# The first layer's 1/rms moved from the projections' input to their output

## The chip, the cores and the metric

The kernel runs on one core of one Trainium2 chip. The metric is the device time of one execution in microseconds; the median of 3 runs of the kernel before is 2711.04 (2710.79 to 2717.03). Everything is fp32 in and out. A core has five engines that run side by side, each with its own in-order stream: PE (TensorE, matrix products), DVE (VectorE), ACT (ScalarE), POOL (GpSimd) and SP, which here only issues DMAs. PE writes its products to PSUM, eight banks of 512 fp32 columns for each of 128 partitions.

## The reference, cut to what matters

A two-layer encoder trunk works on 1024 prompt frames and 64 sample frames of width 1024. Each layer adds a mixer and an FFN to x, and both read a normalised x:

```python
def rmsnorm(x, g):
    xf = x.astype(F32)
    y = xf * lax.rsqrt(jnp.mean(xf * xf, axis=-1, keepdims=True) + EPS) * g.astype(F32)
    return y.astype(x.dtype)

aq, ak, av, bq, bk, bv = split_cols(h @ w_in, AB_SIZES)     # h = rmsnorm(x, g)
```

The first layer's mixer has 4 heads of differential attention and 8 heads of band attention; queries, keys and values of all of them are columns of one projection of h. The 1/rms of a frame is one number per row of h, so it can be multiplied to a row of h @ w_in as well as to a row of x. New keys and values are outputs too.

## The kernel before, in words

Frames lie along the free axis, and model columns along the partitions, so x is 8 tiles of 128 rows by 1088 frames, cut into three chunks of 384, 384 and 320 frames (CH). A fp32 matrix is multiplied in two parts: ACT rounds it to a high part (L235) and DVE or POOL subtracts to get the low part (L236, `split`). One projection of 128 columns over one chunk is then 8 blocks of k times three products (L263 to L265 in `gemm`, L275 in `gemm_steps`, where they can be taken in pieces): high times high, high times low and low times high.

The first layer runs 8 units, one per differential head and one per pair of band heads. Each unit needs its own queries, keys and values: three projections over three chunks. Unit 0's are made in `start`, before any attention; those of units 1 to 7 are made by `proj`, as filler between the attention steps of the unit before, with two PSUM banks in turn. The parts of the normalised x, `hh` and `hl`, stay in SBUF for all of them.

`start` loads x chunk by chunk. For a chunk, `addsq` squares each of the 8 tiles on ACT (L300, L303) and sums them on DVE (L304); `rms` averages over partitions with a product with a constant matrix (L285) and takes 1/rms as exp(-0.5 ln(.)) on ACT (L289 or L291, and L292); `norm` multiplies x by the norm's weight and 1/rms on DVE (L313) and splits the result. The weights of keys and values are issued behind the first chunk's last low part. Then come the projections of a chunk and their unloading: `put_q` writes scaled high parts of the queries on ACT (L351, L352), copies them to the other half of the partitions by DMA and makes low parts on DVE (L356); `new_k` copies PSUM to a staging tile on DVE (L369) and splits it by halves (L332 to L335); `new_v` copies PSUM (L379), transposes on PE (L385) and splits. L487 and L488 are the score products, L499 to L502 the softmax, L520 its scaling, L604 the transposes of the weights.

The program is written in an order, but each engine's stream is laid out by a scheduler that takes ready instructions by its own estimate of times; `issue_after` holds instructions behind a named one. So DMAs and small work can stand far ahead of their place in the text. Buffers are fixed slices of three large tiles, and work that reuses a slice waits for its last reader. The staging tiles share space with the first chunk's sum of squares and with the scratch for squares; the scratch also with the cached keys.

Of the kernel before, what the change touches and what calls it, by code (L numbers as in the profile page):

```python
# [16 lines left out]
F32 = mybir.dt.float32  # L17
AF = mybir.ActivationFunctionType
ALU = mybir.AluOpType
# [5 lines left out]
CH = ((0, 384), (384, 384), (768, 320))  # L25
# [39 lines left out]
F_END = 14464  # L65
F_LF = 14464
F_STG2 = 15808

GROUPS = [(12064 + 2176 * i, 544) for i in range(4)] + [(7360, 544), (38720, 544), (9536, 544), (4416, 544)] + \
    [(R_H + 4 * T * i, T) for i in range(4)] + [(0, 544), (2176, 544)]  # L70
# [74 lines left out]
class Kernel:  # L145
    def __init__(self, tc, M, MR, PS, xTd, oTd, ed, fd, hd, I, O):
# [9 lines left out]
        self.pvp = Ring(PS, [3584], 512)  # L156
        self.mmd = self.mmf
        self.sq = None
        slots = lambda ii: Ring(MR, [R_W + 1024 * i for i in ii], 1024)
        self.raw = Ring(M, [F_RAW, F_RAW + 1024], 1024)  # L160
        self.w_a = slots([0, 1]), slots([2, 3])
# [114 lines left out]
            yield "z", n * 1.25e-3  # L276


    def rms(self, ci, parts=None, to=None):
        nc = self.nc  # L280
        c0, n = CH[ci]
        ms = self.mm.get()[:, :n]
        parts = parts or [ci]
        for p in parts:
            nc.tensor.matmul(ms, self.o1024, self.acc[p][:, :n], start=(p == parts[0]), stop=(p == parts[-1]))  # L285
        r = (self.rb.get() if to is None else to)[:, :n]
        if ci == 0:
            with self.tc.issue_after(self.table("natural_log_exp_and_others")):
                nc.scalar.activation(r, ms, AF.Ln, bias=self.eps)  # L289
        else:  # L290
            nc.scalar.activation(r, ms, AF.Ln, bias=self.eps)  # L291
        self.after_rms = nc.scalar.activation(r, r, AF.Exp, scale=-0.5).ins  # L292
        return r
# [53 lines left out]

    def put_q(self, d, c0, n, ps):
        nc = self.nc
        q0, q1, l0, l1 = (t[:, c0:c0 + n] for t in (*d["q"], *d["ql"]))  # L350
        nc.scalar.activation(q0[0:64], ps[0:64], AF.Copy, scale=SCALE)  # L351
        nc.scalar.activation(q1[64:128], ps[64:128], AF.Copy, scale=SCALE)  # L352
        self.dma(q0.bitcast(F32)[64:128], q0.bitcast(F32)[0:64])
        self.dma(q1.bitcast(F32)[0:64], q1.bitcast(F32)[64:128])
        for b, q, ql in ((0, q0, l0), (64, q1, l1)):
            nc.vector.scalar_tensor_tensor(ql[b:b + 64], ps[b:b + 64], SCALE, q.bitcast(F32)[b:b + 64], op0=ALU.mult, op1=ALU.subtract)  # L356

    def new_rows(self, c0, n, sg, outs, keep):

# [6 lines left out]

    def new_k(self, d, c0, n, ps, outs, keep, sub=None):
        sg = self.stg.get()[:, :n]
        self.nc.vector.tensor_copy(sg, ps)  # L369
        npr = min(n, TP - c0)  # L370
        self.put_k(d["k"], c0, ps[:, :npr], sg[:, :npr], npr, sub)
        if npr < n:
            self.put_k(d["ks"], PAST, ps[:, npr:n], sg[:, npr:n], TS, sub)
        self.new_rows(c0, n, sg, outs, keep)

    def new_v(self, d, c0, n, ps, pair, outs, keep):
        nc = self.nc
        sg = self.stg.get()[:, :n]
        nc.vector.tensor_copy(sg, ps)  # L379
        npr = min(n, TP - c0)  # L380
        nt = npr // 128
        yield "t", 0.0
        pt = self.ptp.get()
        for t in range(nt):
            nc.tensor.transpose(pt[:, t * 128:t * 128 + 128], sg[:, t * 128:t * 128 + 128], self.ident)  # L385
        self.put_v(d["v"], 8, c0 // 128, nt, 128, pt[:, :npr], pair, nc.vector)
        if npr < n:
            nc.tensor.transpose(pt[0:64, 384:512], sg[:, npr:n], self.ident)
            self.put_v(d["vs"], 3, 2, 1, 64, pt[:, 384:512], pair, nc.vector)
        self.new_rows(c0, n, sg, outs, keep)  # L390
# [40 lines left out]
    def start(self, d, wq, wk, wv, pair, outs):  # L431
        nc, I = self.nc, self.I
# [2 lines left out]
        rings = tuple(Ring(self.MR, [R_W + 2048 * i + o for i in range(2)] + [R_Q[1] + o], 1024) for o in (0, 1024))  # L435
        ring = Ring(self.PS, [512 * i for i in range(5)], 512)

        def loadx(ci):
            c0, n = CH[ci]
            for k in range(8):  # L440
                self.dma(self.x[k][ci], I["xT"][k * 128:k * 128 + 128, c0:c0 + n])

        loadx(0)
        w = [self.loadw(wq, rings)]
        loadx(1)
        for k in range(8):
            self.addsq(0, k, self.x[k][0])
        last = self.norm(0, 0, 1, (nc.gpsimd, nc.gpsimd))
        with self.tc.issue_after(last.ins):
            w.append(self.loadw(wk, rings, sub=nc.vector))  # L450
            w.append(self.loadw(wv, rings))
        loadx(2)
        self.dma(self.ident, I["ident"])
        self.dma(self.causal, I["causal"])
        for ci, (c0, n) in enumerate(CH):
            p = [ring.get()[:, :n] for _ in range(3)]
            for i in range(3):
                self.gemm(p[i], w[i], c0, n)
                if i == 0 and ci < 2:
                    self.norm(ci + 1, 0, 2 if ci == 0 else None)  # L460
            self.put_q(d, c0, n, p[0])
            if ci == 0:
                self.cached_k(d, ckT)
# [1049 lines left out]
    def layer_cd(self, pending):  # L1513
        nc, I, O = self.nc, self.I, self.O
        W = I["cdw"]
        self.lastu = 3
        rest = self.recurrent(pending, self.qkv_views(0), W[0], W[4], I["cckT"][0], (O["c_kT"][0], O["sc_kT"][0]), 0)
        self.dg = Ring(self.M, [F_BIAS + 2688 + 128 * i for i in range(3)], 128)
        units = [(W[u], W[4 + u], W[8 + u], True,
# [108 lines left out]
```

## Time and profile before

| | us |
|---|---|
| median of 3 runs | 2711.04 |
| profiled execution, its own time | 2712.83 |
| span of that execution | 2711.0 |
| PE busy in the span | 2596.9 (96%) |
| DVE busy | 1325.7 (49%) |
| ACT busy | 1196.2 (44%) |
| POOL busy | 1155.1 (43%) |
| mean granted PE clock | 0.987 |

The span runs from the first to the last instruction in the profile; the execution's own time lies a little around it. A row of a grouped view reads: line, engine, operation, what is written <- what is read, shape, count | busy time, mean ns of one | idle time of the engine just before, with what ended it. A timeline row begins with start and duration in us, and a bracket gives the idle time before it and what ended it. "banks" is PSUM; "arena" and "split_arena" are the two SBUF tiles.

### The profile page before, as it was taken

The page shows a single profiled execution, that of the slowest core. Times are in us where ns is not written, and L with a number is a line of the kernel's source. Part 1 is how long each engine was busy: PE and PEld are TensorE (multiplying, and loading weights), DVE is VectorE, ACT ScalarE, POOL GpSimd, SP SyncE. Part 2 cuts the span into 40 slices and gives each one's busy share as a digit, 9 for nine tenths or more (in the row PEclk, how much of TensorE's full clock was granted, in tenths as well). Part 3 has the DMA queues.
Part 4 walks back from the last instruction along what each step waited for, and adds up shares of the span by engine and source line. Part 5 has one row for each costly group of instructions (what it writes and reads, how often), then busy time and mean ns, then how long its engine had stood idle before and what let it go on. Part 6 is the DMA issues. An engine that isn't in the chain of part 4 may idle for free. (4 is left out here: it accounts for less than half of the span.)

```text
span 2711.0 us, 44897 instructions
## 1 busy us (share of the span) xinstructions
PE 2596.9 (96%) x17610; PEld 2525.3 (93%) x17610; DVE 1325.7 (49%) x2763; ACT 1196.2 (44%) x2373; POOL 1155.1 (43%) x939
## 2 busy tenths in 40 slices
PE   6999999999999999999998979999999999999998
PEld 5899999889899999999998969988989999999998
DVE  7666666777432333422156557777743233242214
ACT  5666667764322233311135566686432323331112
POOL 5222222324666666422335433343366666641230
PEclk9999999999999999999999989999999999999999
DMA  6222222342222222442232342234322122244211
GB/s 204 73 71 69 78 63 62 104 151 92 83 95 66 81 72 87 141 154 72 74 105 60 52 80 79 78 123 150 100 86 97 64 82 70 88 141 153 72 55 67
DMA packets 115109, 250.21 MB, mean 92 GB/s; under 512 B 21432, under 2 KB 70848, under 8 KB 114896
## 3 DMA queue, kind: packets, MB, share of 16 engines
q1 hardware_dynamic: 114896, 247.33, 29.9%
q8 instruction: 138, 2.26, 0.4%
q14 instruction: 75, 0.61, 0.1%
HBM read 179.09 MB, written 65.43 MB: 90 GB/s over the span
## 5 line engine op out<-in xcount | busy, mean ns | idle before, releaser
L236 POOL TENSOR_TENSOR split_arena<-arena,split_arena 128x512 fp32r<-128x512 f32 (+5 forms) x501 | 756.7, 1522 | 1181.6 <-ACT split_arena L235 1091.7
L1070 PE MATMUL banks<-split_arena 128*128 128x272 f32 x7392 | 944.5, 290 | 23.3 <-ACT arena L1077 8.0
L1070 PEld LDWEIGHTS banks<-split_arena 128*128 128x128 f32 x7392 | 937.6, 190 | 30.0 <-ACT arena L1077 8.8
L235 ACT ACTIVATE split_arena<-arena 128x512 fp32r<-128x512 f32 (+10 forms) x664 | 458.8, 707 | 1020.3 <-PE banks L1070 291.9
L275 PE MATMUL banks<-split_arena 128*128 128x384 f32 (+1 forms) x3384 | 632.0, 333 | 3.4 <-POOL split_arena L236 2.3
L275 PEld LDWEIGHTS banks<-split_arena 128*128 128x128 f32 x3384 | 558.5, 189 | 10.9 <-POOL split_arena L236 2.9
L1182 PE MATMUL banks<-split_arena 128*128 128x384 f32 (+1 forms) x1056 | 345.1, 327 | 2.2 <-DVE arena L1148 1.4
L1184 PE MATMUL banks<-split_arena 128*128 128x384 f32 (+1 forms) x1056 | 344.4, 326 | 0.0
L1183 PE MATMUL banks<-split_arena 128*128 128x384 f32 (+1 forms) x1056 | 344.2, 326 | 0.0
L236 DVE TENSOR_TENSOR split_arena<-banks,split_arena 128x512 fp32r<-128x512 f32 (+4 forms) x312 | 167.4, 541 | 89.9 <-ACT split_arena L235 87.2
L499 DVE CUSTOM_DVE_ANT_0 arena<-banks,arena 128x384 f32<-128x384 f32 (+4 forms) x368 | 175.5, 493 | 56.4 <-PE banks L488 40.2
L1182 PEld LDWEIGHTS banks<-split_arena 128*128 128x128 f32 x1056 | 198.2, 188 | 3.6 <-DVE arena L1148 2.0
L1183 PEld LDWEIGHTS banks<-split_arena 128*128 128x128 f32 x1056 | 198.2, 188 | 0.3
L1184 PEld LDWEIGHTS banks<-split_arena 128*128 128x128 f32 x1056 | 198.2, 188 | 0.0
L235 ACT ACTIVATE split_arena<-banks 128x512 fp32r<-128x512 f32 (+4 forms) x312 | 146.7, 476 | 97.4 <-PE banks L604 43.3
L236 DVE TENSOR_TENSOR split_arena<-arena,split_arena 128x1088 fp32r<-128x1088 f32 (+8 forms) x163 | 154.0, 952 | 70.9 <-ACT split_arena L235 70.4
L1081 DVE TENSOR_TENSOR arena<-banks,arena 128x544 f32<-128x544 f32 (+1 forms) x46 | 32.2, 700 | 301.7 <-PE banks L1070 301.7
L501 ACT ACTIVATE arena<-arena 128x640 f32<-128x640 f32 (+8 forms) x216 | 156.3, 724 | 47.0 <-DVE arena L499 45.5
L1214 DVE TENSOR_TENSOR arena<-banks,arena 128x384 f32<-128x384 f32 (+1 forms) x96 | 51.1, 534 | 250.4 <-PE banks L1184 250.2
L604 PE MATMUL banks<-arena 128*128 128x128 f32 (+2 forms) x828 | 135.4, 276 | 18.8 <-DVE arena L520 11.5
L604 PEld LDWEIGHTS banks<-arena 128*128 128x128 f32 (+2 forms) x828 | 96.4, 141 | 37.7 <-DVE arena L520 15.1
L263 PE MATMUL banks<-split_arena 128*128 128x384 f32 (+1 forms) x312 | 106.7, 344 | 16.7 <-ACT arena L1399 10.0
(165 smaller groups left out, 3076.4 us busy)
## 6 DMA issues: line engine op xcount, KB each, us to landing
arena<-in_w_dram SPq DMA_DIRECT2D x120, 512.0 KB, 3.6
h_spill<-arena SPq DMA_DIRECT2D x22, 1088.0 KB, 4.2
arena<-h_spill SPq DMA_DIRECT2D x44, 544.0 KB, 4.4
arena<-in_abw_dram SPq DMA_DIRECT2D x24, 512.0 KB, 3.6
arena<-in_cdw_dram SPq DMA_DIRECT2D x20, 512.0 KB, 3.6
x_spill<-arena SPq DMA_DIRECT2D x48, 192.0 KB, 1.9
arena<-x_spill SPq DMA_DIRECT2D x16, 544.0 KB, 4.9
arena<-in_w_dram SPq DMA_DIRECT2D x19, 384.0 KB, 3.2
```

The lines of the kernel that those rows point to most:

```text
L235: self.hi = self.nc.scalar.activation(hi, x, AF.Copy).ins
L236: lo = sub.tensor_tensor(lo, x, hi.bitcast(F32), op=ALU.subtract)
L263: nc.tensor.matmul(ps, wh[:, k], hh[k][:, c0:c0 + n], start=(k == ks[0]), stop=False)
L275: self.pe = self.nc.tensor.matmul(ps, x[:, k], y[k][:, c0:c0 + n], start=a and i == 0, stop=z and i == 2).ins
L499: nc.vector.tensor_tensor_reduce(o, p, t, -1.0, low, ALU.add, ALU.min, to)
L501: nc.scalar.activation(sb, sb, AF.Exp, bias=st[:, 0:1], scale=-1.0, accum_out=st[:, 1:2])
L604: nc.tensor.transpose(pt[:r, t * nq + s * m:t * nq + s * m + m], src, self.ident[:m, :m])
L1070: last = nc.tensor.matmul(bank[:, p], l[:, k], r[:, k, x], start=first and i == 0, stop=k == 3 and i == 2, skip_group_check=True)
L1182: nc.tensor.matmul(ps, wh, h[:, c0:c0 + n], start=j == j0, stop=False)
L1183: nc.tensor.matmul(ps, wh, lo[:, c0:c0 + n], start=False, stop=False)
L1184: nc.tensor.matmul(ps, wl, h[:, c0:c0 + n], start=False, stop=j == j1 - 1)
L1214: nc.vector.tensor_tensor(xs, pss[ci], xs, op=ALU.add)
```

## The change

In the first layer, `hh` and `hl` become the parts of x times the norm's weight, without 1/rms. `parts` makes them: ACT writes the rounded product with a per-partition scale, DVE makes the low part in one scalar_tensor_tensor. 1/rms of each chunk is kept in a tile `rs` of its own (128 x 1088, at F_R, the place of the first buffer for raw FFN weights) and multiplied when a projection leaves PSUM: in place in PSUM for queries, in place of the copy for keys and values (`unload`). The key parts are then made from the staged copy. This holds for all 8 units; the second layer sets `rs` to None and unloads as before.

`start` is rearranged: weights of queries, half of x, weights of keys, the other half, weights of values, then the second and third chunk; the weights' low parts go to DVE instead of POOL. In the first chunk, the products of queries and of keys over the first half of x precede those over the second half. Sums of squares and 1/rms come, in the text, after a chunk's projections; the first 1/rms no longer has an activation-table load held before it.

```diff
+F_R = 14464
...
+        self.rs = {c0: self.v(F_R + c0, n) for c0, n in CH}
...
     def put_q(self, d, c0, n, ps):
         nc = self.nc
+        if self.rs:
+            nc.vector.tensor_tensor(ps, ps, self.rs[c0], op=ALU.mult)
...
+    def unload(self, sg, c0, ps):
+
+        if self.rs:
+            self.nc.vector.tensor_tensor(sg, ps, self.rs[c0], op=ALU.mult)
+        else:
+            self.nc.vector.tensor_copy(sg, ps)
...
     def new_k(self, d, c0, n, ps, outs, keep, sub=None):
         sg = self.stg.get()[:, :n]
-        self.nc.vector.tensor_copy(sg, ps)
+        self.unload(sg, c0, ps)
+        if self.rs:
+            ps = sg
...
     def new_v(self, d, c0, n, ps, pair, outs, keep):
-        nc.vector.tensor_copy(sg, ps)
+        self.unload(sg, c0, ps)
...
-        def loadx(ci):
+        def loadx(ci, ks=range(8)):
...
+        def parts(ci, ks=range(8)):
+
+            c0, n = CH[ci]
+            for k in ks:
+                x, g = self.x[k][ci], self.pcol(k)
+                hi, lo = self.hh[k][:, c0:c0 + n], self.hl[k][:, c0:c0 + n]
+                nc.scalar.activation(hi, x, AF.Copy, scale=g)
+                nc.vector.scalar_tensor_tensor(lo, x, g, hi.bitcast(F32), op0=ALU.mult, op1=ALU.subtract)
+
+        w = [self.loadw(wq, rings, sub=nc.vector)]
+        loadx(0, range(4))
+        parts(0, range(4))
+        w.append(self.loadw(wk, rings, sub=nc.vector))
+        loadx(0, range(4, 8))
+        parts(0, range(4, 8))
+        w.append(self.loadw(wv, rings, sub=nc.vector))
         loadx(1)
-        for k in range(8):
-            self.addsq(0, k, self.x[k][0])
-        last = self.norm(0, 0, 1, (nc.gpsimd, nc.gpsimd))
-        with self.tc.issue_after(last.ins):
-            w.append(self.loadw(wk, rings, sub=nc.vector))
-            w.append(self.loadw(wv, rings))
         loadx(2)
...
             p = [ring.get()[:, :n] for _ in range(3)]
-            for i in range(3):
+            if ci == 0:
+
+                for ks in (range(4), range(4, 8)):
+                    for i in range(2):
+                        for _ in self.gemm_steps(p[i], w[i], c0, n, ks=ks, first=ks[0] == 0, last=ks[0] == 4):
+                            pass
+            for i in range(2 if ci == 0 else 0, 3):
                 self.gemm(p[i], w[i], c0, n)
-                if i == 0 and ci < 2:
-                    self.norm(ci + 1, 0, 2 if ci == 0 else None)
+            for k in range(8):
+                self.addsq(ci, k, self.x[k][ci])
+            if ci < 2:
+                parts(ci + 1)
+            self.rms(ci, to=self.rs[c0], table=False)
             self.put_q(d, c0, n, p[0])
...
     def layer_cd(self, pending):
+        self.rs = None
```

More of the change, by code (lines that the diff above doesn't have):

```diff
@@ L276, in gemm_steps, with rms @@
             yield "z", n * 1.25e-3
-    def rms(self, ci, parts=None, to=None):
+    def rms(self, ci, parts=None, to=None, table=True):
         nc = self.nc
@@ L286, in rms @@
         r = (self.rb.get() if to is None else to)[:, :n]
-        if ci == 0:
+        if ci == 0 and table:
             with self.tc.issue_after(self.table("natural_log_exp_and_others")):
@@ L436, in start @@
         ring = Ring(self.PS, [512 * i for i in range(5)], 512)
-        def loadx(ci):
+        def loadx(ci, ks=range(8)):
             c0, n = CH[ci]
-            for k in range(8):
+            for k in ks:
                 self.dma(self.x[k][ci], I["xT"][k * 128:k * 128 + 128, c0:c0 + n])
-        loadx(0)
-        w = [self.loadw(wq, rings)]
-        loadx(1)
-        for k in range(8):
-            self.addsq(0, k, self.x[k][0])
-        last = self.norm(0, 0, 1, (nc.gpsimd, nc.gpsimd))
-        with self.tc.issue_after(last.ins):
-            w.append(self.loadw(wk, rings, sub=nc.vector))
-            w.append(self.loadw(wv, rings))
+        def parts(ci, ks=range(8)):
+            c0, n = CH[ci]
+            for k in ks:
+                x, g = self.x[k][ci], self.pcol(k)
[9 more added lines that the diff above has]
+        w.append(self.loadw(wv, rings, sub=nc.vector))
+        loadx(1)
         loadx(2)
```

## The prediction

> **What bounds the kernel now.** I read the page first, then busy time by stretch, then who keeps PE waiting in the opening, then the timeline of the opening, then grouped durations.
>
> ```profile
> span 2711.0 us, 44897 instructions
> PE 2596.9 (96%) x17610; PEld 2525.3 (93%) x17610; DVE 1325.7 (49%) x2763; ACT 1196.2 (44%) x2373; POOL 1155.1 (43%) x939
> ```
>
> PE is busy 96% of the span, so time can be won only where PE is idle or slow. Two stretches follow: the opening up to the first attention score, and layer 0's attention units up to its output projection. Columns after the length are busy time on PE, PE's weight loads, DVE, ACT, POOL, then granted clock and DMA.
>
> ```profile
> 0.00:76.50 76.50, 50.67 (x228) 43.76 (x229) 55.84 (x89) 42.47 (x84) 41.87 (x38) 0.93 0.66 196
> 76.50:640.00 563.50, 550.48 (x3556) 521.55 (x3557) 374.59 (x1066) 378.03 (x853) 145.92 (x137) 1.00 0.28 83
> ```
>
> PE idles 76.5 - 50.7 = 25.8 us of the opening and 13.0 us of the 563.5 us behind it. The change rebuilds the opening and only adds work behind it. PE's waits in the opening:
>
> ```profile
> PE banks L285 <- DVE arena L304: 11.1, 1, 11.1
> PE banks L263 <- ACT split_arena L235: 6.8, 3, 4.1
> PE banks L264 <- POOL split_arena L236: 2.8, 6, 0.9
> PE banks L264 <- DVE split_arena L236: 2.3, 2, 1.9
> ```
>
> It waits first for the sum of squares (L304), then for high parts (L235) and low parts (L236) made from the normalised x: norm, parts and products stand in a row. The opening on PE:
>
> ```profile
> 16.82 0.69 PE L263 MATMUL banks<-split_arena 128*128 128x384 f32 x1 [4.11 <-ACT split_arena L235]
> ...
> 26.01 0.53 PE L265 MATMUL banks<-split_arena 128*128 128x384 f32 x1
> ...
> 26.33 0.53 PE L263 MATMUL banks<-split_arena 128*128 128x384 f32 x1
> ...
> 36.08 0.33 PE L263 MATMUL banks<-split_arena 128*128 128x384 f32 x1
> 36.26 0.33 PE L264 MATMUL banks<-split_arena 128*128 128x384 f32 x1
> ...
> 74.04 0.31 PE L264 MATMUL banks<-split_arena 128*128 128x320 f32 x1
> 74.19 0.31 PE L265 MATMUL banks<-split_arena 128*128 128x320 f32 x1
> 76.53 0.33 PE L487 MATMUL banks<-split_arena 128*64 128x320 f32 x1 [2.03 <-issue]
> ```
>
> The first product of the projections starts at 16.8 us, the last at 74.2, the first score at 76.5. Near 26 us starts lie 0.32 us apart, later 0.17 to 0.18 (0.15 for the narrow third chunk). At the quick pace the 144 + 72 products need 144 x 0.173 + 72 x 0.147 = 35.5 us; they are spread over 57.
>
> **Part 1: the opening.** The diff removes 24 passes of x times weight times 1/rms (L313) with the wait for 1/rms before them. High and low parts come straight from x: ACT writes x times weight (8 per chunk), DVE makes the low part in one pass and POOL makes none. The DMAs on SP change order to queries' weights, half of x, keys' weights, the other half, values' weights, second and third chunk of x; keys' and values' weights no longer wait behind the last norm pass. The values' weights reuse the first raw buffer, so their DMA waits on SP until the first split is done, and all DMAs queued later wait with it: the second and third chunk of x.
>
> Arrival first. Sizes and rate:
>
> ```profile
> arena<-in_abw_dram SPq DMA_DIRECT2D x7, 512.0 KB, 3.6
> arena<-in_xT_dram SPq DMA_DIRECT2D x16, 192.0 KB, 5.2
> arena<-in_xT_dram SPq DMA_DIRECT2D x8, 160.0 KB, 3.8
> ...
> 11.00:17.00 6.00, 1.83 (x3) 0.69 (x3) 2.90 (x5) 4.23 (x8) 2.50 (x2) 1.00 0.86 277
> ```
>
> Three weight blocks and x are 3 x 512 + 16 x 192 + 8 x 160 = 5888 KB, 6.03 MB: 21.8 us at 277 GB/s. With the first issue at 1.2 us and about 3 us from issue to landing the last byte is there near 26 us. The queries' weights and half of x (1280 KB) are there at about 9, everything for chunk one (3072 KB) at 15.5. After two split passes for the values' weights, their 24 products end at 22 to 26, by pace; I take 24. Chunks two and three then run 72 x 0.173 + 72 x 0.147 = 23 us, to 47. Waits of PE inside this I estimate at 2 us: 49.
>
> The tail is new. Before, the third 1/rms was made early; now its products stand behind the third chunk's, and no query, key or value leaves PSUM before it. Rows of the old tail:
>
> ```profile
> L291 ACT ACTIVATE arena<-banks,arena 128x320 f32<-128x320 f32 x1 | 0.5, 527 | 0.3 <-POOL split_arena L236 0.3
> L292 ACT ACTIVATE arena<-arena 128x320 f32<-128x320 f32 x1 | 0.5, 472 | 0.0
> L285 PE MATMUL banks<-arena 128*128 128x320 f32 x2 | 0.7, 434 | 0.0
> 71.02 0.49 DVE L369 COPY arena<-banks 128x320 f32<-128x320 f32 x1 [1.36 <-PE banks L265]
> ```
>
> Root products, Ln and Exp take 0.7 + 0.53 + 0.47 = 1.7 us; from the keys' unloading (71.0) to the first score (76.5) it took 5.5. So 49 + 7.2 = 56.2 us for the first score.
>
> Now the same by DVE, which could bind instead:
>
> ```profile
> L313 DVE SCALAR_TENSOR_TENSOR arena<-arena 128x384 f32<-128x384 f32 x16 | 12.3, 802 | 1.1 <-POOL split_arena L236 0.9
> L304 DVE TENSOR_TENSOR arena<-arena 128x384 f32<-128x384 f32 x14 | 10.4, 744 | 7.2 <-ACT arena L303 6.8
> L313 DVE SCALAR_TENSOR_TENSOR arena<-arena 128x320 f32<-128x320 f32 x8 | 7.5, 970 | 1.9 <-POOL split_arena L335 1.3 <-issue 0.7
> L304 DVE TENSOR_TENSOR arena<-arena 128x320 f32<-128x320 f32 x7 | 6.1, 877 | 0.8 <-ACT arena L303 0.5
> L335 DVE TENSOR_TENSOR split_arena<-arena,split_arena 64x256 fp32r<-64x256 f32 x1 | 2.5, 2475 | 0.0
> L236 DVE TENSOR_TENSOR split_arena<-arena,split_arena 128x1024 fp32r<-128x1024 f32 x1 | 1.2, 1211 | 0.0
> L369 DVE COPY arena<-banks 128x384 f32<-128x384 f32 x2 | 1.1, 553 | 0.0
> L236 POOL TENSOR_TENSOR split_arena<-arena,split_arena 128x384 fp32r<-128x384 f32 x12 | 14.0, 1184 | 13.1 <-ACT split_arena L235 13.1
> ```
>
> A pass over 384 columns takes 0.55 us, over 320 0.49 (L369 at 71.02); L313 and L304 average 0.74 to 0.97 where POOL subtracts beside them. At the undisturbed prices: weights' low parts 3 x 1.21 = 3.6; low parts of x 16 x 0.55 + 8 x 0.49 = 12.7; adds of squares 14 x 0.55 + 7 x 0.49 = 11.1; queries (a multiply and two half-width passes of the same length per chunk) 6 x 0.55 + 3 x 0.49 = 4.8; unloading keys and values 3.2; values' split 1.7; third chunk's key subtractions about 4.6 at the slow row's size (2.5 each, narrow ones less); the small derived constants about 2. Together 43.7 us. Starting when the first weights land, at about 5.5, that ends at 49 without an idle moment; at the old opening's busy share (55.8 / 76.5 = 73%) it needs 60. PE's chain, 56, lies between, and I take 56: **20.5 us gained**. Bounds: 27 (DVE never idle), and 13.3 us less than 20.5 if passes stay at the disturbed means (37.1 instead of 23.8 for L313 and L304's counts).
>
> POOL loses the 16 subtractions of x and two of weights in the opening. The Trainium skill, SBUF — State Buffer, section Who interferes with whom, says that a VectorE instruction with two SBUF inputs contends with a GpSimd instruction that reads SBUF. The rows (0.55 against 0.74 to 0.97) agree; by this rule the low price would hold and the first score stands at 56, without it the high one would, and the sum would be 13.3 us worse.
>
> **Part 2: seven more units.** The parts stay unnormalised, so units 1 to 7 multiply too. Keys and values: a multiply replaces a copy. Queries: 21 multiplies are added, written back to PSUM.
>
> ```profile
> L879 DVE TENSOR_TENSOR arena<-banks,arena 128x384 f32<-128x384 f32 x16 | 8.5, 549 | 8.7 <-PE banks L275 8.7
> L369 DVE COPY arena<-banks 128x384 f32<-128x384 f32 x14 | 7.8, 555 | 2.1 <-PE banks L275 1.8
> L379 DVE COPY arena<-banks 128x384 f32<-128x384 f32 x14 | 7.8, 557 | 17.6 <-PE banks L275 17.6
> ...
> PE banks L604 <- DVE arena L520: 5.2, 6, 2.7
> ```
>
> A two-input pass from PSUM (0.549) costs what the copy does (0.556): keys and values 0. Its key high parts now read the unloaded copy instead of PSUM, one pass later, but PSUM comes free earlier; 0. Queries: 14 x 0.55 + 7 x 0.49 = 11.1 us on DVE. No row shows DVE writing PSUM; the nearest is L879. DVE is idle 563.5 - 374.6 = 189 us there, which is the cover. The multiplies cost between 0 (covered) and 11.1 (each holds PE for its length). PE's longest wait on DVE there totals only 5.2 us, so I take 2, near the low end.
>
> **Part 3: the 1/rms storage** lies where the first weight block of the FFN lands:
>
> ```profile
> 54.45 0.61 SPq L188 DMA_DIRECT2D arena<-in_w_dram  x1
> ```
>
> That DMA (512 KB) is issued at 54 us, 600 us ahead of its use, and must now wait for unit 7's last value. Taken 0, since the output projection still lies between; 3.6 us (the landing time of such a block) if that cover were gone.
>
> **Sum**, against the profiled execution: its span is 2711.0, its own time 2712.83, 1.8 around the span; the median of the runs is 2711.04, 1.8 below that time. 2711.0 - 20.5 + 2 = 2692.5 of span, 2694.3 with what lies around it, 2692.5 as a median. I say **2693**.
>
> **Rivals.**
> A. *The opening goes further*: DVE's 49 us or the arrival (26 + 23 = 49) alone sets it. For: PE may start the next unit's queries in the tail. Against: the new tail of 7 us. 2711 - 27 + 0 = 2684. Chance 0.14.
> B. *DVE binds*: scratch for squares shares space with staging, so adds for a chunk wait for the chunk before to be stored, and passes stay long. The gain is 20.5 less 8 to 13 (that 13.3 or a good half of it), say 10 left: 2711 - 10 + 2 = 2703; half of it below 2702.9. Chance 0.17.
> C. *PE stays at the slow pace*: each gap brings the 0.32 us spacing back, as at 16.8 to 26.6. All products slow: 144 x 0.32 + 72 x 0.267 = 65.3 us (0.267 is 0.32 x 320/384) after a start at 8, so 73 us, almost the old 76.5: 2708 to 2710. Against: chunks two and three depend on parts made ahead. Chance 0.06. The Trainium skill, TensorE: Matmul & The Clock Gate, section Part 1: The HAM clock gate, has half rate after an idle window of about 3.4 us; the spacings 0.32 and 0.17 agree with the two rates.
> D. *Slower*: the query multiply heads DVE's in-order queue and waits for its products, as L379 does (17.6 us idle for 14, 1.26 each), and scores queued behind it hold PE. 21 x (1.26 + 0.55) = 38 us: 2711 - 20.5 + 38 = 2729. It decides once each multiply costs PE over 20.5 / 21 = 0.98 us. Against: 189 us of idle DVE. Chance 0.08.
> E. *It doesn't do what it says*: starting keys on half of x wins nothing since later arrivals and the third 1/rms set the end, and the gap reappears there: 2711. Chance 0.05.
>
> **How the numbers follow.** The forecast (2686 to 2700) has 0.50. A measurement tells about 0.3%, 8.1 us, from no change. Faster than 2702.9: 0.50 + 0.14 + half of B, 0.09, = 0.73. Within: the rest of B, C and E, 0.19. Slower: D, 0.08. The range runs from 2682, just under A, to 2709, which takes in B and C; it leaves out D, E and the part of A below it, in all under 2 in 10.
>
> **What would show it.** First product at 7 to 9 us, first score at 52 to 60; L304 and the low parts of x near 0.55 us; POOL idle beside them; units 1 to 7 as long as before within 2 us, with 21 multiplies near 0.55. I am wrong if the first score comes after 65 us, if the opening's DVE busy time stays above 50 us, or if attention stretches by more than 5.

## The result and the profile after

The changed kernel takes 2693.56 us (median of 4 runs, 2692.35 to 2697.17) against 2714.03 for the kernel before, timed beside it: a ratio of 0.9929, interval 0.9914 to 0.9943. It is 0.7% faster; 2693 had been forecast.

First the page of the changed kernel. Its span is 20.3 us shorter, DVE's busy time hardly moves, and POOL does 22.6 us less.

```profile
span 2690.7 us, 44860 instructions
PE 2589.7 (96%) x17610; PEld 2521.9 (94%) x17610; DVE 1320.6 (49%) x2781; ACT 1196.7 (44%) x2372; POOL 1132.5 (42%) x921
```

Next, busy time by stretch (columns as in the prediction: length, busy time on PE, PE's weight loads, DVE, ACT and POOL, granted clock, DMA share, GB/s): the time up to the first score, and from there to the first product of the first FFN, of the kernel before,

```profile
76.50:663.00 586.50, 573.42 (x3710) 544.26 (x3711) 397.59 (x1090) 388.83 (x871) 165.54 (x147) 1.00 0.27 83
```

and of the changed kernel, where the first 60 us and the second stretch are shown.

```profile
0.00:60.00 60.00, 47.28 (x252) 45.17 (x253) 42.05 (x88) 41.32 (x84) 18.36 (x20) 0.94 0.80 250
...
60.50:644.40 583.90, 569.30 (x3686) 538.49 (x3684) 403.97 (x1108) 391.02 (x870) 166.85 (x147) 1.00 0.28 83
```

The first score now comes at 60.5 us instead of 76.5 (16.0 earlier) and the first FFN starts at 644.4 instead of 663.0 (18.6 earlier). The remaining 1.7 us of the span arise behind it, where nothing was changed, and are no more than its scatter: from the first FFN product to the end of the span the kernel before took 2048.0 us, the changed kernel 2046.3, and the same changed kernel in another run 2042.2. Over all the kernels below this stretch ran from 2040.6 to 2051.9. So two landmarks, the first score and the start of the first FFN, separate the kernels better than the total.

Now PE's timeline in the opening of the changed kernel. L278 and L266 to L268 are the projections' products, L288 the mean of squares, L518 the first score; L463 and L464 make the high and low parts of x, L307 adds squares.

```profile
6.62 0.69 PE L278 MATMUL banks<-split_arena 128*128 128x384 f32 x1 [6.62 <-ACT split_arena L463]
7.91 10.10 PE L278 MATMUL banks<-split_arena 128*128 128x384 f32 x47 [0.60 <-DVE split_arena L464]
...
21.84 0.33 PE L268 MATMUL banks<-split_arena 128*128 128x384 f32 x1
22.01 0.81 PE L288 MATMUL banks<-arena 128*128 128x384 f32 x2
...
46.90 0.31 PE L268 MATMUL banks<-split_arena 128*128 128x320 f32 x1
52.60 1.43 PE L288 MATMUL banks<-arena 128*128 128x320 f32 x2 [5.40 <-DVE arena L307]
53.37 5.38 PE L278 MATMUL banks<-split_arena 128*128 128x384 f32 x15
58.59 0.38 PE L399 MATMUL banks<-arena 128*128 128x128 f32 x2
58.73 1.98 PE L278 MATMUL banks<-split_arena 128*128 128x384 f32 x10
60.55 0.30 PE L518 MATMUL banks<-split_arena 128*64 128x320 f32 x1
```

From 7.9 to 46.9 us PE runs without a wait worth naming. Then it stands still for 5.4 us, for the third sum of squares. After that it does 25 recorded products of the next unit's queries before the first score. That is work which the kernel before did later, so the gain that counts is more than 16.0: the first unit's output norm (a product that comes once per group of queries) starts at 76.4 us instead of 96.9, 20.5 earlier. Its rows in the kernel before (L541) and in the changed kernel (L572) give minimum, median and maximum in ns, then the first and the last start in us:

```profile
L541 PE MATMUL banks<-arena x40: 275/378/483, 96.9 to 322.6; 128*128 128x256 f32 x32, 128*128 128x64 f32 x8
L572 PE MATMUL banks<-arena x40: 275/378/483, 76.4 to 302.1; 128*128 128x256 f32 x32, 128*128 128x64 f32 x8
```

What held the third sum of squares shows in ACT's timeline (L306 squares): it waited for a DMA that stores the second chunk's values.

```profile
47.16 0.47 ACT L306 ACTIVATE arena<-arena 128x320 f32<-128x320 f32 x1 [4.43 <-DMA out_a_vT_dram<-arena]
48.90 1.52 ACT L306 ACTIVATE arena<-arena 128x320 f32<-128x320 f32 x3 [1.27 <-DVE arena L307]
```

The squares' scratch and the values' staging tile are the same slice of SBUF. That is the mechanism of rival B, with a price of about 5 us of PE's time here; the run with free scratch below tests it.

Groups of DVE's instructions up to 76 us, in the changed kernel: the passes that make low parts (L464) and add squares (L307) average 0.55 to 0.71 us each, where norm passes and adds averaged 0.74 to 0.97 before. (Busy time is less than count times mean, since passes overlap a little.)

```profile
L464 DVE SCALAR_TENSOR_TENSOR split_arena<-arena,split_arena 128x384 fp32r<-128x384 f32 x16 | 8.9, 612 | 0.0
L307 DVE TENSOR_TENSOR arena<-arena 128x384 f32<-128x384 f32 x14 | 8.6, 612 | 0.5
L307 DVE TENSOR_TENSOR arena<-arena 128x320 f32<-128x320 f32 x7 | 5.0, 713 | 6.8 <-ACT arena L306 6.4
L464 DVE SCALAR_TENSOR_TENSOR split_arena<-arena,split_arena 128x320 fp32r<-128x320 f32 x8 | 3.9, 545 | 0.0
```

### The profile page after: what moved, and what is told of

The parts are those of the page before. It is cut to its first block, busy times and chain, and to the rows that moved or that the text cites. A ratio compares the mean times of both kernels' runs of the same rounds, so it can differ in the third digit from the quotient of the medians.

```text
span 2690.7 us, 44860 instructions
## 1 busy us (share of the span) xinstructions
PE 2589.7 (96%) x17610; PEld 2521.9 (94%) x17610; DVE 1320.6 (49%) x2781; ACT 1196.7 (44%) x2372; POOL 1132.5 (42%) x921
## 4 chain that ended last, share of the span: by engine, by line
PE 77%; DVE 8%; ACT 6%; DMA 5%; issue 2%; POOL 2%; SPq 0%; DVEq 0%; ACTq 0%; POOLq 0%
PE banks L1101 33%; PE banks L278 14%; PE banks L1215 6%; PE banks L1213 6%; PE banks L1214 6%; PE banks L635 3%; ACT split_arena L238 2%; DVE split_arena L239 2%; PE banks L518 2%; PE banks L519 1%; PE banks L560 1%; PE banks L561 1%; DMA arena<-o_spill 1%; POOL split_arena L239 1%; ACT arena L532 1%
## 5 line engine op out<-in xcount | busy, mean ns | idle before, releaser
L239 POOL TENSOR_TENSOR split_arena<-arena,split_arena 128x512 fp32r<-128x512 f32 (+6 forms) x483 | 733.0, 1529 | 1150.9 <-ACT split_arena L238 1054.0
L238 ACT ACTIVATE split_arena<-arena 128x512 fp32r<-128x512 f32 (+9 forms) x640 | 446.4, 715 | 1007.1 <-PE banks L1101 293.4
L278 PE MATMUL banks<-split_arena 128*128 128x384 f32 (+1 forms) x3432 | 645.8, 335 | 11.8 <-ACT split_arena L463 6.6
L278 PEld LDWEIGHTS banks<-split_arena 128*128 128x128 f32 x3432 | 570.1, 190 | 20.8 <-ACT split_arena L463 6.6
L1213 PE MATMUL banks<-split_arena 128*128 128x384 f32 (+1 forms) x1056 | 345.0, 327 | 2.5 <-DVE arena L1179 1.7
L1215 PE MATMUL banks<-split_arena 128*128 128x384 f32 (+1 forms) x1056 | 344.5, 326 | 0.0
L1214 PE MATMUL banks<-split_arena 128*128 128x384 f32 (+1 forms) x1056 | 344.2, 326 | 0.0
L518 PE MATMUL banks<-split_arena 128*128 128x256 f32 (+3 forms) x312 | 113.8, 367 | 7.4 <-POOL split_arena L337 7.4
```

The lines of the kernel that those rows point to most:

```text
L238: self.hi = self.nc.scalar.activation(hi, x, AF.Copy).ins
L239: lo = sub.tensor_tensor(lo, x, hi.bitcast(F32), op=ALU.subtract)
L278: self.pe = self.nc.tensor.matmul(ps, x[:, k], y[k][:, c0:c0 + n], start=a and i == 0, stop=z and i == 2).ins
L518: nc.tensor.matmul(ps[:, :mw], qd[:, q0:q0 + m], kk[:, k0 + s:k0 + s + mw], start=True, stop=False)
L1213: nc.tensor.matmul(ps, wh, h[:, c0:c0 + n], start=j == j0, stop=False)
L1214: nc.tensor.matmul(ps, wh, lo[:, c0:c0 + n], start=False, stop=False)
```

## The experiments

All are edits of the changed kernel unless said otherwise. For each stands the ratio to the kernel before with its 95% interval, the first score and the start of the first FFN, both in us from the span's start. The changed kernel has 60.5 and 644.4; the two landmarks of the kernel before are 76.5 and 663.0.

| run | ratio (interval) | first score | first FFN |
|---|---|---|---|
| changed kernel again | 0.9924 (0.9910 to 0.9937) | 61.3 | 645.5 |
| old kernel, new order of loads | 0.9992 (0.9983 to 1.0001) | 74.2 | 663.8 |
| old order of loads | 0.9962 (0.9948 to 0.9976) | 69.1 | 654.3 |
| keys after all of the queries | 0.9930 (0.9916 to 0.9944) | 59.7 | 643.7 |
| half of x's low parts over POOL | 0.9956 (0.9943 to 0.9970) | 68.7 | 654.3 |
| weights' low parts on POOL | 0.9943 (0.9929 to 0.9957) | 63.9 | 648.5 |
| no query multiply in units 1 to 7 | 0.9923 (0.9910 to 0.9935) | 61.3 | 642.5 |
| one more pass on queries | 0.9915 (0.9902 to 0.9929) | 60.6 | 643.1 |
| three more passes on queries | 1.0019 (1.0010 to 1.0028) | 60.3 | 665.7 |
| free scratch | 0.9916 (0.9903 to 0.9930) | 56.2 | 642.0 |
| free scratch, 1/rms earlier | 0.9923 (0.9910 to 0.9935) | 53.1 | 639.2 |
| ... one projection earlier still | 0.9916 (0.9904 to 0.9929) | 51.4 | 641.7 |

**The changed kernel again.** No edit.

> The changed kernel as it is, on the same chip as the three beside it. Its ratio to the kernel before is 0.991 to 0.994 as when it was first timed; first score at 60 to 61 us, the first products of the first FFN at 643 to 646.

The ratio and the start of the FFN lie where they were expected, the first score 0.3 us above. The landmarks differ by 0.8 and 1.1 us between two runs of the same kernel; from this one pair, that is how finely they can be read.

**The order of loads alone, in the kernel before.**

```diff
-        def loadx(ci):
+        def loadx(ci, ks=range(8)):
...
-        loadx(0)
-        w = [self.loadw(wq, rings)]
+        w = [self.loadw(wq, rings, sub=nc.vector)]
+        loadx(0, range(4))
+        w.append(self.loadw(wk, rings, sub=nc.vector))
+        loadx(0, range(4, 8))
+        w.append(self.loadw(wv, rings, sub=nc.vector))
         loadx(1)
...
-        with self.tc.issue_after(last.ins):
-            w.append(self.loadw(wk, rings, sub=nc.vector))
-            w.append(self.loadw(wv, rings))
```

> The kernel before (norm at the input), with the new order of loads alone: weights of queries first, half of x, weights of keys, the other half, weights of values, with the weights' low parts on DVE and no hold behind the last low part of the first chunk. My theory (the chain squares, 1/rms, norm, parts, products is what binds the old opening, not the loads): first score at 72 to 77 us, time within 4 us of the kernel before. Rival (the loads' order made most of the gain): first score at 62 to 66, 10 to 15 us faster, a ratio of 0.995.

By itself the new order gains little as long as the norm stands ahead of the products: 2.3 us at the first score, and nothing in the total (0.9992). The start of the FFN is no fair landmark for this run. The output projection's first sum still comes 2.2 us earlier than in the kernel before (549.9 against 552.1), and from 600 to 664 us this execution shows a granted clock of 0.92 where the kernel before shows 1.00. PE's waits in its opening:

```profile
PE banks L285 <- DVE arena L304: 14.5, 1, 14.5
PE banks L263 <- ACT split_arena L235: 5.7, 3, 2.4
```

The mean of squares now waits 14.5 us instead of 11.1: weights are loaded ahead of x, and the first chunk's squares need all of it.

**The old order of loads, in the changed kernel.**

```diff
-        w = [self.loadw(wq, rings, sub=nc.vector)]
-        loadx(0, range(4))
-        parts(0, range(4))
-        w.append(self.loadw(wk, rings, sub=nc.vector))
-        loadx(0, range(4, 8))
-        parts(0, range(4, 8))
-        w.append(self.loadw(wv, rings, sub=nc.vector))
-        loadx(1)
+        loadx(0)
+        w = [self.loadw(wq, rings, sub=nc.vector)]
+        parts(0)
+        loadx(1)
+        w.append(self.loadw(wk, rings, sub=nc.vector))
+        w.append(self.loadw(wv, rings, sub=nc.vector))
         loadx(2)
```

> The changed kernel (1/rms at the output) with the old order of loads: all of the first chunk of x, then weights of queries, second chunk, weights of keys and values, third chunk. My theory: the first product comes 4 to 6 us later (12 instead of 6.6) and the keys' and values' products later still, but the wait for the third 1/rms hides part; first score at 62 to 66, 2 to 6 us slower than the changed kernel, 0.994 to 0.995. Rival (the loads' order made most of the gain): 10 us or more slower, 0.997 to 1.0.

The first product starts at 12.45 us, and the FFN 9.9 us later than in the changed kernel; I had expected 2 to 6 of slowdown, and the rival's 10 or more lies nearer.

```profile
12.45 1.01 PE L278 MATMUL banks<-split_arena 128*128 128x384 f32 x2 [12.45 <-ACT split_arena L238]
```

By the start of the FFN the four combinations are 663.0 (neither), 663.8 (order alone), 654.3 (1/rms at the output alone) and 644.4 (both); by the first score they are 76.5, 74.2, 69.1 and 60.5. 1/rms at the output, with the weights' low parts on DVE and without the hold on the keys' and values' weights, is worth 8.7 us by itself. The order is worth 9.9 more on top of it, and 2.3 at most alone. The reason that I see is that only parts that don't wait for the squares can be made before the whole first chunk is there; no run tests it apart. Nor does a run separate, within the 8.7 us, the shorter chain from POOL's 16 subtractions of x that go with the norm.

**Keys after all of the queries.**

```diff
             if ci == 0:
 
-                for ks in (range(4), range(4, 8)):
-                    for i in range(2):
-                        for _ in self.gemm_steps(p[i], w[i], c0, n, ks=ks, first=ks[0] == 0, last=ks[0] == 4):
-                            pass
-            for i in range(2 if ci == 0 else 0, 3):
+                pass
+            for i in range(3):
```

> The changed kernel with the first chunk's keys begun only when its queries are done (products of all 8 blocks of queries, then keys, then values), loads as in the change. My theory: PE runs at the arrival of x either way, and the tail behind the third chunk decides; 0 to 2 us slower than the changed kernel, first score at 60 to 62. Rival (beginning keys early keeps PE in work and at its full clock): 3 to 6 us slower.

Both landmarks lie within 0.8 us of the changed kernel's. To begin keys on half of x, which the change's description names, is worth nothing that can be told here.

**Half of the low parts of x over POOL.** For every second k the product of x and weight is written out by DVE, and POOL subtracts.

```diff
+        half = Ring(self.M, [F_R + T, F_RB], 384)
...
-                nc.vector.scalar_tensor_tensor(lo, x, g, hi.bitcast(F32), op0=ALU.mult, op1=ALU.subtract)
+                if k % 2:
+                    t = half.get()[:, :n]
+                    nc.vector.tensor_scalar(t, x, g, None, op0=ALU.mult)
+                    nc.gpsimd.tensor_tensor(lo, t, hi.bitcast(F32), op=ALU.subtract)
+                else:
+                    nc.vector.scalar_tensor_tensor(lo, x, g, hi.bitcast(F32), op0=ALU.mult, op1=ALU.subtract)
```

> The changed kernel with every second low part of x made in two steps, a multiply on DVE into scratch and a subtraction on POOL, so DVE has as many passes as in the change and POOL works beside them as in the kernel before. By the contention that I named: the opening's passes of DVE over 384 columns go from about 0.55 to 0.65 or more on the mean, DVE is busy 4 us or more longer in the opening, first score at 62 to 67, 2 to 6 us slower than the changed kernel. Rival (the slow means of the kernel before had another cause): means stay at 0.55 to 0.58 and the time within 2 us.

It costs 9.9 us up to the FFN, more than I had set. DVE's groups, up to 76 us (L471 is the low part in one pass, L468 the written product):

```profile
L307 DVE TENSOR_TENSOR arena<-arena 128x384 f32<-128x384 f32 x14 | 9.3, 666 | 1.6 <-ACT arena L306 1.1
L471 DVE SCALAR_TENSOR_TENSOR split_arena<-arena,split_arena 128x384 fp32r<-128x384 f32 x8 | 5.5, 702 | 0.0
L468 DVE TENSOR_SCALAR arena<-arena 128x384 f32<-128x384 f32 x8 | 5.5, 693 | 0.0
L471 DVE SCALAR_TENSOR_TENSOR split_arena<-arena,split_arena 128x320 fp32r<-128x320 f32 x4 | 3.9, 1010 | 0.0
```

The means over 384 columns rise from 0.61 to 0.67 and 0.70, the narrow low parts from 0.55 to 1.01 us. Up to the first score DVE is busy 47.03 us against the 42.05 of the changed kernel, 5.0 more, as I had set (4 or more). That is not the whole of the 9.9 us: this edit also adds waits of its own, for scratch and for POOL, and how the rest divides is not shown.

**The weights' low parts on POOL**, for queries and values, as in the kernel before; nothing is added here.

```diff
-        w = [self.loadw(wq, rings, sub=nc.vector)]
+        w = [self.loadw(wq, rings)]
...
-        w.append(self.loadw(wv, rings, sub=nc.vector))
+        w.append(self.loadw(wv, rings))
```

> The changed kernel with the low parts of the queries' and the values' weights on POOL, as before. A pass over 1024 columns takes POOL 2.3 to 2.5 us and DVE 1.2. My theory: low part of the queries' weights 1.1 us later, but the first three products need high parts too; chunk one ends 1 to 2 us later, first score within 2 us of the changed kernel, 0.992 to 0.994 of the kernel before. Rival (POOL's subtractions hold DVE's passes): first score 3 us later or more.

My number was too small, and the rival holds: the first score comes 3.4 us later and the FFN 4.1. DVE's timeline in this run and POOL's two subtractions,

```profile
6.69 3.96 DVE L464 SCALAR_TENSOR_TENSOR split_arena<-arena,split_arena 128x384 fp32r<-128x384 f32 x4 [1.79 <-ACT split_arena L463]
...
19.07 9.57 DVE L464 SCALAR_TENSOR_TENSOR split_arena<-arena,split_arena 128x384 fp32r<-128x384 f32 x12
...
6.29 2.36 POOL L239 TENSOR_TENSOR split_arena<-arena,split_arena 128x1024 fp32r<-128x1024 f32 x1 [1.42 <-ACT split_arena L238]
...
19.27 2.67 POOL L239 TENSOR_TENSOR split_arena<-arena,split_arena 128x1024 fp32r<-128x1024 f32 x1 [10.62 <-DMA arena<-in_xT_dram]
```

against the same passes in the changed kernel, where POOL is idle from 4.9 to 24.7 us:

```profile
7.24 2.20 DVE L464 SCALAR_TENSOR_TENSOR split_arena<-arena,split_arena 128x384 fp32r<-128x384 f32 x4
...
18.71 6.03 DVE L464 SCALAR_TENSOR_TENSOR split_arena<-arena,split_arena 128x384 fp32r<-128x384 f32 x12
```

Four equal passes take 3.96 us instead of 2.20 with one POOL subtraction beside them. Twelve take 9.57 instead of 6.03 with one large and three small ones, though they are no more work (a row can merge both widths: here five of 384 and seven of 320 columns, in the changed kernel six and six). So the price of POOL beside them is 1.8 and 3.5 us. It does not fall on every pass alike. All 24 low parts of x, with minimum, median and maximum in ns, in this run and in the changed kernel:

```profile
L464 DVE SCALAR_TENSOR_TENSOR split_arena<-arena,split_arena x24: 541/610/2761, 6.7 to 32.9; 128x384 fp32r<-128x384 f32 x16, 128x320 fp32r<-128x320 f32 x8
L464 DVE SCALAR_TENSOR_TENSOR split_arena<-arena,split_arena x24: 542/611/615, 7.2 to 31.1; 128x384 fp32r<-128x384 f32 x16, 128x320 fp32r<-128x320 f32 x8
```

The median doesn't move. The first of the four passes takes 2.37 us, to 9.06, and one of the twelve takes 2.76, to 22.4; each ends 0.4 us behind the POOL subtraction beside it (8.65 and 21.94). The other three of the four take 0.60 to 0.61; beside the three small subtractions three narrow passes take 1.02 to 1.03. So a pass is held for about as long as POOL's instruction runs, and the rest run free. The Trainium skill, SBUF — State Buffer, section Who interferes with whom, has such pairs contend, and these rows agree. Moving two subtractions from POOL to DVE is worth about 4 us of the gain.

**No query multiply in units 1 to 7, and one and three passes more.** The first leaves out the 1/rms of those units' queries. The diff is that of three more passes; with one more, 1 stands for the 3.

```diff
         if self.rs:
             nc.vector.tensor_tensor(ps, ps, self.rs[c0], op=ALU.mult)
+            for _ in range(0 if self.first else 3):
+                nc.vector.tensor_scalar(ps, ps, 1.0, None, op0=ALU.mult)
```

> The changed kernel, with the 21 query multiplies of units 1 to 7 left out (their queries are then not divided by rms; all else stays). My theory (covered by idle DVE): the attention units take 0 to 3 us less, a ratio of 0.992 to 0.993. Rival (each multiply holds PE for its length): 11 us less, 0.989. Rival of the slower side (each costs the wait in the queue too): 20 us and more, 0.985.

> The changed kernel, with one more pass of DVE in place over each of the 21 query tiles of units 1 to 7 (times 1.0; 11 us of DVE work). Three more cost 21 us up to the first FFN, nearly all in units 1 to 3; leaving the multiply out won 1.9. If the cost grows with the length of a pass: 7 us. If it sets in once a query bank is held longer than the products between allow (my theory): 0 to 4 us, first FFN at 644 to 648. If the multiplies of the change sit at that edge already: over 7.

> The changed kernel, with three more passes of DVE in place over each of the 21 query tiles of units 1 to 7 (times 1.0; 33 us of DVE work in all). My theory (DVE has 180 us idle in the units): the time grows by 2 to 8 us, 0.994 to 0.996 of the kernel before. Rival (a pass on the queries holds PE for its length): 33 us more, 1.005. If 21 multiplies already use up the cover, 15 us or more.

Without the multiply the FFN starts 1.9 us earlier, with one more pass 1.3 us earlier than in the changed kernel: both are near the 1.1 us between two runs of it, so the multiplies' price is not told from nothing. If each pass had its price, the start would come later with every one added; it doesn't. Three more passes cost 21.3 us, where I had set 2 to 8. That lies where I had put the case that the 21 multiplies already use up the cover (15 us or more), but the run with one more pass speaks against that case. Nearly all of it falls in units 1 to 3: the last output norm of a differential head starts at 323.3 us instead of 302.1. PE's waits there, in the run with three more passes, from 60 to 325 us, and one of its stretches:

```profile
PE banks L639 <- DVE arena L546: 7.7, 5, 2.2
PE banks L279 <- DVE split_arena L364: 5.2, 4, 1.4
PE banks L522 <- DVE arena L534: 0.5, 1, 0.5
...
140.00:150.00 10.00, 6.44 (x26) 5.79 (x27) 8.57 (x18) 5.44 (x13) 3.85 (x2) 0.63 0.37 102
150.00:160.00 10.00, 10.00 (x60) 9.66 (x60) 7.08 (x23) 6.43 (x12) 0.82 (x1) 0.86 0.07 24
```

The products of the projections (L279) wait for the queries' low parts (L364), the last reader of their PSUM bank, and the transposes (L639) wait for the softmax work on DVE (L546, which combines a differential head's two softmaxes) that now stands behind the added passes. Together these are 13.4 us of waits, where the changed kernel has 1.9 from 60 to 325 us. The other 9.0 us are PE's busy time, which grows from 239.8 to 248.8 us for the same products; they go with the clock, 0.95 in the mean instead of 1.00 and 0.63 and 0.86 in these two stretches. Idle DVE in the mean says little about the price of a pass: one or two vanish, four do not; three were not run.

**Free scratch.**

```diff
+        tmp, self.tmp = self.tmp, Ring(self.M, [F_TMP[2], F_R + T], 384)
...
+        self.tmp = tmp
         self.derived()
```

> The changed kernel with the scratch for squares of the opening in two slots that nothing else uses, so that the adds of the third chunk need not wait until the staged values of the second chunk are stored. My theory (the shared scratch holds the third 1/rms and with it the tail): PE's 5.4 us wait before the third root products falls under 1 us, the first score comes at 55 to 57 us instead of 60.5, and the time falls by 3 to 5 us, a ratio near 0.991 to the kernel before. Rival (the tail is held by DVE and ACT work in any case, the wait only shows it): the wait moves to another place, first score at 59 to 61, time unchanged within 1 us, 0.993.

The 5.4 us wait is gone, and the first score comes 4.3 us earlier. What precedes it now, on PE's timeline, is the copy of the third chunk's queries:

```profile
56.19 0.33 PE L520 MATMUL banks<-split_arena 128*64 128x320 f32 x1 [2.65 <-DMA split_arena<-split_arena]
```

The wait ahead of it, 2.65 us, stands in the bracket. The FFN starts 2.4 to 3.5 us earlier (against two runs of the changed kernel). The median is 2687.96 us and the ratio among the lowest of the table, but its interval overlaps the changed kernel's. So the shared scratch is shown as the cause of the wait; that the program gets faster by it is shown by the landmark alone.

**1/rms earlier**, on top of the free scratch: the squares and root products of the second and third chunk ahead of the values' products.

```diff
             for i in range(2 if ci == 0 else 0, 3):
+                if i == 2:
+                    for k in range(8):
+                        self.addsq(ci, k, self.x[k][ci])
+                    if ci < 2:
+                        parts(ci + 1)
+                    if ci:
+                        self.rms(ci, to=self.rs[c0], table=False)
                 self.gemm(p[i], w[i], c0, n)
-            for k in range(8):
-                self.addsq(ci, k, self.x[k][ci])
-            if ci < 2:
-                parts(ci + 1)
-            self.rms(ci, to=self.rs[c0], table=False)
+            if ci == 0:
+                self.rms(ci, to=self.rs[c0], table=False)
```

> As the run with free scratch, and the squares and 1/rms of the second and third chunk stand, in the text, ahead of the values' products, so that the third 1/rms is ready while PE still multiplies. My theory (the tail of 1/rms, multiply and key parts behind the last product is exposed): first score at 49 to 53 us, time 7 to 11 us below the changed kernel, a ratio of 0.989 to 0.990. Rival (PE only takes the next unit's queries earlier in the tail already, so the tail costs nothing): first score moves but the units behind start with the same backlog, time within 2 us of the run with free scratch alone.

In a third version the squares and root products of the third chunk stand one projection earlier still (`if i == (1 if ci == 2 else 2)`).

> As the run with free scratch and early 1/rms, with the third chunk's squares and root products one projection earlier still, behind its queries' products. There the third root products began at 45.0 us, and the score waited 2.8 us for the copy of the third queries, 6 us behind PE's last product. My theory (this tail is exposed): root products at 41 to 42, first score at 48 to 51, the first FFN begins 6 to 9 us before that of the changed kernel, time 0.988 to 0.991 of the kernel before. Rival (PE or DVE work behind the first score sets the pace now): the FFN begins no earlier than in the run before it, 5 us ahead of the changed kernel.

The first score moves to 53.1 and 51.4 us, 7.4 and 9.1 earlier than in the changed kernel, but the FFN starts only 5.2 and 2.7 earlier; 7 to 11 (of total time) and 6 to 9 had been expected. In the second of them, PE's stretch from the first score to the FFN (columns as above) grows by most of what the opening loses:

```profile
51.40:641.70 590.30, 575.32 (x3711) 544.78 (x3712) 405.03 (x1112) 392.53 (x871) 167.44 (x147) 1.00 0.28 85
```

That is 590.3 us against 583.9, with 575.3 of PE's time busy against 569.3: 25 more products are recorded here, as many as the next unit's queries that filled the old tail. So a good part of the tail behind the last product was not lost. The last version bears its rival out. The one before it lies between theory and rival by the FFN's start, and with the rival by its total (2689.87 us, 1.9 from the run with free scratch alone). How much of the difference between the two is the clock, which falls behind the wait in one and not in the other (last section), is not shown. None of the three versions is told from the changed kernel by its total; the free scratch alone gives as much as any.

## Why the prediction was right

**The opening**: 20.5 us of gain were forecast for it. The first score gained 16.0, and with the next unit's queries done ahead the first output norm gained 20.5. That I had the size right rests on two errors that cancel, which is luck. The first score was set at 56.2 and came at 60.5. The failing term is "waits of PE inside this I estimate at 2 us", with a tail of 7.2: PE had no waits between 7.9 us and its last product, but 5.4 us behind it, for squares held by the shared scratch, and from the start of the last product to the first score it took 13.6 us. I had put that mechanism into rival B as a wide loss and not into the tail, where it took its 4 to 5 us. In return I had left the next unit's queries to rival A, and PE did them in the tail.

The closeness of the total is luck in part too. The span was forecast at 2692.5 us and came at 2690.7. Up to the FFN's start 18.5 us of gain were forecast (20.5 less 2) and 18.6 measured; the other 1.7 us arose behind it. By medians the gain is 20.5 us where 18 were forecast, since the kernel before came out at 2714.03 instead of 2711.04 with a fourth execution.

**The steps of PE's chain** held. Arrival was faster than I set: 277 GB/s was the mean of a stretch of 6 us in the old opening that also holds slack. Over 10 to 14 us the kernel before and the changed kernel show:

```profile
10.00:14.00 4.00, 1.65 (x2) 0.50 (x2) 0.56 (x1) 3.97 (x7) 1.08 (x1) 1.00 1.04 357
10.00:14.00 4.00, 3.90 (x20) 3.58 (x20) 3.85 (x7) 4.00 (x8) 0.00 (x0) 1.00 1.02 384
```

Chunk one ended at 22.0 instead of 24, without a wait for loads behind 7.9 us, and chunks two and three, with root products and transposes between, took 24.9 instead of 23: the last product starts at 46.9, against the 47 that I had worked out before waits. The first product starts at 6.6, just ahead of the 7 to 9 that I gave.

**DVE's sum**, 43.7 us, measured 42.1 in the first 60 us. Its terms fit less well: the adds of squares took 13.6 us instead of 11.1, and the third chunk's key subtractions 1.3 instead of 4.6, for which I had taken the row of 2.475 us. The undisturbed price of a pass held: 0.55 each (2.20 / 4) when POOL is idle. The disturbed means that I set against it, 0.74 to 0.97, are not what a pass costs beside POOL but a mixture, as the run with the weights' low parts on POOL shows; in the kernel before, L313 has a median of 0.61 us and a longest pass of 2.73. Rival B's price for staying at those means, 8 to 13 us, is near to the 9.9 of the run with half of the low parts over POOL, but only 5.0 of them are DVE's busy time.

**The new units**: 2 us were taken; leaving out the multiply saved 1.9, which is at the edge of what can be told. From the first output norm to the output projection's first sum the units took 455.2 us before (96.9 to 552.1) and 456.9 after (76.4 to 533.3), 1.7 more. The open price, DVE writing its result to PSUM in place, was that of a read alone:

```profile
L354 DVE TENSOR_TENSOR banks<-banks,arena x24: 486/549/567, 24.7 to 463.4; 128x384 f32<-128x384 f32 x16, 128x320 f32<-128x320 f32 x8
```

Its median is 0.549 us (minimum, median and maximum are given), as for the nearest row of before. Of rival D's mechanism the run with three more passes shows a part, softmax work queued behind the added passes that holds PE; the other part there, the PSUM bank held longer, D didn't name. With one multiply neither shows.

**The 1/rms storage** cost nothing: the FFN's first weight block is issued at 515 us instead of 54, and from the output projection's first sum to the first FFN product it takes 111.1 us (533.3 to 644.4) against 110.9 (552.1 to 663.0).

**The other rivals.** C, the slow pace for all, didn't come about: from 17.8 us on products start 0.17 us apart (0.15 in the third chunk), with no gap before 47. E, that early keys win nothing, is right in that clause and wrong in its conclusion: the halves are worth nothing, but the order of loads that goes with them is worth 9.9 us once 1/rms is off the path. Its other clause, that the gap reappears at the third 1/rms, came true with 5.4 us.

## What to carry to other kernels

A factor that is one number per row can be taken out of a product's input and multiplied to its output; what that wins is read off the chain ahead of the first product, and it grows when the loads are then put into the order in which the products can begin. Its price is a pass per output tile, and whether that pass is free is decided by how long it holds the PSUM bank and what stands behind it on its engine, not by the idle share: one and two showed no cost here, four cost 21 us. Where another engine reads beside a pass, look at the median and the longest pass and not at the mean: here single passes were held for a whole instruction of POOL, and the others cost nothing more. A wait at the end of a stage is only lost as far as the engine has nothing else ready; here 4.3, 7.4 and 9.1 us of an earlier first score left 2.4, 5.2 and 2.7.

## What the runs showed that was not expected

Waits of a few microseconds can bring PE's clock down behind them. In the changed kernel the one gap of 5.4 us is followed by a stretch at a mean clock of 0.63:

```profile
47.00:53.00 6.00, 0.60 (x3) 0.40 (x2) 4.51 (x6) 1.88 (x4) 2.87 (x3) 0.89 0.38 107
53.00:60.50 7.50, 7.50 (x29) 7.05 (x29) 3.97 (x10) 3.58 (x9) 1.78 (x2) 0.63 0.66 192
```

And with three more passes, waits of 2.2 and 1.3 us inside ten us go with a clock of 0.63; it is down to 0.50 from 143 us, ahead of the second of them. The Trainium skill, TensorE: Matmul & The Clock Gate, section Part 1: The HAM clock gate, asks for an idle window of about 3.4 us; the first case agrees, and in the second no single recorded wait is that long; where they differ, the measurement counts.

The runs with free scratch show the same behind single waits. With 1/rms one projection earlier still, PE waits 2.05 us and the clock falls to 0.69 in the mean behind it; with free scratch alone, 2.65 us are followed by 0.65. With 1/rms earlier, 2.81 us are followed by 1.00. In this order:

```profile
51.39 0.33 PE L524 MATMUL banks<-split_arena 128*64 128x320 f32 x1 [2.05 <-DVE split_arena L337]
51.40:55.00 3.60, 3.60 (x17) 3.40 (x18) 2.16 (x9) 2.53 (x7) 1.46 (x2) 0.69 0.83 243
56.20:60.00 3.80, 3.80 (x15) 3.46 (x16) 2.13 (x9) 3.18 (x10) 0.73 (x1) 0.65 0.38 106
53.08 0.33 PE L524 MATMUL banks<-split_arena 128*64 128x320 f32 x1 [2.81 <-DMA split_arena<-split_arena]
53.10:57.00 3.90, 3.90 (x25) 3.82 (x26) 2.52 (x10) 2.92 (x9) 1.05 (x2) 1.00 0.71 220
```

So the length of a wait alone does not decide in these runs whether the clock falls; what does, they don't show.

The other surprise is the loads: the opening's DMA reached 384 GB/s over 4 us, where the stretch that I had used showed 277. The old opening had reached 357 over the same 4 us, so the stretch that I chose is most of that difference.
